# Folding eight heads' sums of 16 tokens on VectorE and by transfers instead of on TensorE

## The chip, the cores and the metric

The kernel runs on one core of a Trainium2 chip. The metric is the device time of one execution in microseconds (us). TensorE is the matrix engine, VectorE (DVE in the rows of the profile), ScalarE (ACT) and GpSimd (POOL) work on tiles of 128 partitions, and the DMA engines move data. SyncE (SP) and GpSimd issue most transfers. The engines run at once and wait for each other by semaphores; each works through its own instructions in the order in which they were written.

## The reference

One decoder layer over 256 tokens of width 1024. The first half (a projection, a retention branch, an attention branch, a gated merge) gives a residual stream x1. The second half adds to it a retrieval of single-neuron experts, and only this part matters here:

```python
q = (ht @ w_q).reshape(T, PEER_HEADS, 2, half)                  # 8 heads
...                                                             # top 16 of 128 * 128 experts for each head
def one_chunk(args):
    hc, ec, gc = args
    u = u_tab[ec]                                               # rows of a table of 16384 experts
    a = jax.nn.gelu(jnp.einsum('td,thkd->thk', hc, u), approximate=False)
    return jnp.einsum('thk,thkd->td', gc * a, v_tab[ec])        # sum over 8 heads and 16 experts of each
...
x = x + peer(h2, ...)
```

For each token, 8 heads x 16 experts give 128 rows of `peer_v` (1024 numbers each), which are summed with weights and added to x1.

## The kernel before

The kernel computes most tokens densely: a first product takes all 16384 rows of `peer_u` against the tokens, in 128 chunks of 128 rows; a second product multiplies the weights (zero where an expert was not chosen) with all rows of `peer_v`, again in 128 chunks. Some tokens are handled by gathering just the rows that they need. For the second product these are 64 tokens whose rows are summed in a tile `vacc`, and 16 more tokens whose rows are summed in a tile `accx`. This leaves `ND` = 176 tokens to the second product.

In `accx` the 128 partitions are 8 heads x 16 tokens: partition 16 h + i holds the sum over the 16 experts that head h chose for token i. Each `accx` step gathers one row per partition (an indirect DMA issued by GpSimd, line 1033) and adds it with a weight on VectorE (line 1119). The sums of the 8 heads remain to be added across partitions. TensorE does that: line 1348 multiplies each of the 8 column blocks of `accx` with `pick`, a 128 x 16 matrix of ones at the rows of each token, which gives the 16 tokens' sums as 16 more columns of the second product's result.

The second product (line 1320 on) is one loop over chunks c = 0 to 127. In its iteration c, in this order, the program

- asks SyncE for the next chunks of `peer_v` (512 KB each, into `raw_ring`, which holds 6),
- prepares chunk c + 2: ScalarE rounds it to `rhi` (line 147), VectorE takes the rest `rlo` = chunk - `rhi` (line 148), and for each second chunk the same is done for the weights in `cw` (lines 1256 and 1257),
- lets TensorE multiply chunk c: for each of 8 blocks of 128 columns one matmul of `rhi` (line 1316) and one of `rlo` (line 1317), into 8 banks of PSUM (named `side` or `acc`), where the sums stay over all chunks,
- takes 0.65 of a gather step: GpSimd issues the gather of one set of rows, and VectorE adds the oldest set that was gathered (six sets are in flight).

In six pairs of chunks (12 and 13, 32 and 33, 52 and 53, 72 and 73, 92 and 93, 112 and 113), called plain here, the chunk is not split: one matmul per block (line 1314), nothing to prepare.

At c = 123 all gather sums are done, the rows of x1 are fetched back (lines 1340 to 1346) and line 1348 runs. For the last two chunks the loop goes block by block: when a block is complete, ScalarE and VectorE add its two halves (lines 1360 and 1361), TensorE turns it back to token order (1366 and 1367), VectorE adds x1 (1368 and 1369), and the output is stored. In the tile `r0b`, which collects tokens 64 to 127, rows 48 to 63 are the 16 tokens of `accx`.

The order on each engine is simply that of the program; nothing reorders it later.

Of the kernel before, what the change touches and what calls it, by code (L numbers as in the profile page):

```python
# [11 lines left out]
F32 = mybir.dt.float32  # L12
# [6 lines left out]
AF = mybir.ActivationFunctionType  # L19
OP = mybir.AluOpType  # L20
AX = mybir.AxisListType

P = 128
S = 256
NT = S // P
D = 1024
KC = D // P
# [3 lines left out]
NG = 64  # L31
NXP = 16
# [3 lines left out]
NA = S - NG - NX  # L36
ND = S - NG - NXP * NXV
# [12 lines left out]
TOPK = 16  # L50
HELD = [0, 1, 2, 8, 14, 21] + list(range(26, 62, 6))
HELD0 = 14
NPRE = 16
STEP = 7
PRE0 = 20
# [6 lines left out]
NJ = NP // 2  # L62
NU = NJ + NX
NV = NJ + NXP * NXV
# [11 lines left out]
def layer_kernel(ctx, tc, x, mix_norm_g, w_in, ret_w_branch, moba_q_gain, moba_k_gain, moba_w_branch,  # L76
                 rel_bias, w_out, ffn_norm_g, peer_w_q, peer_sub_keys, peer_u, peer_v,
                 c_rope, c_decay, c_col, c_bucket, out, dbg=None):
    nc = tc.nc
    V, A, G, T = nc.vector, nc.scalar, nc.gpsimd, nc.tensor  # L80
    ctx.enter_context(tc.manual_schedule())

    cp = ctx.enter_context(tc.tile_pool(name="cp", bufs=1))
# [13 lines left out]
    def side():  # L97
        return psum.tile([P, 512], F32, name="side", bufs=4)
# [64 lines left out]
    x1d = dr.tile([P, NT, D], F32, name="x1d")  # L163
# [4 lines left out]
    hTf = cp.tile([P, KC, NA], F32, name="hTf")  # L168
    hh = [hp_.tile([P, 4, S], F32R, name="hh", bufs=2) for _ in range(2)]
    hl = [hp_.tile([P, 4, S], F32R, name="hl", bufs=2) for _ in range(2)]  # L170

    turned = dr.tile([NPRE, P, D], F32, name="turned")
    ident = cp.tile([P, P], F32, name="ident")
# [515 lines left out]
    def load_any(i):  # L689

        if sk_at <= i < sk_at + 2:
            r = raw_tile().rearrange("p (j i) -> p j i", j=H)
            nc.sync.dma_start(r, peer_sub_keys[0].rearrange("h c n d -> n (h c) d")[:, H * (i - sk_at):H * (i - sk_at + 1), :])
            sk_raw.append(r)
            return
        i -= 2 * (i >= sk_at)
        if i < len(pieces):
            load(i)
        elif i < len(pieces) + NK:
            c = i - len(pieces)  # L700
            if c in HELD:
                return
            if early_chunk(c):
                u_raw[c] = raw_tile()
                nc.sync.dma_start(u_raw[c], turned[c // STEP])
            elif c in TURN:
                u_raw[c] = raw_tile()
                load_quarters(nc.sync, u_raw[c], c)
            else:
                u_raw[c] = load_rows(peer_u, c)  # L710
        elif i < len(pieces) + 2 * NK:
            v_raw[i - len(pieces) - NK] = load_rows(peer_v, i - len(pieces) - NK)
# [4 lines left out]
    def load_to(i):  # L717
        while state["loaded"] < i + AHEAD + 2 * (i + AHEAD > sk_at):
            load_any(state["loaded"])
            state["loaded"] += 1  # L720
# [19 lines left out]
    def early_chunk(c):  # L740
        return c % STEP == STEP - 1 and c // STEP < NPRE

# [11 lines left out]
    def early_turns(i):  # L754

        m, step = divmod(i - PRE0, PERIOD)
        if step == 0 and -1 <= m < NPRE - 1:
            load_quarters(nc.scalar, early[0][(m + 1) % 2], STEP * (m + 1) + STEP - 1)
        if 0 <= m < NPRE:
            if step < 2:  # L760
# [33 lines left out]
    for t in range(NT):  # L794
        for q in range(2):
            c = slice(512 * q, 512 * (q + 1))
# [3 lines left out]
            p = side()  # L800
# [4 lines left out]
    for q in range(2):  # L805
        for t in range(NT):
            n = slice(t * P, (t + 1) * P)
            A.activation(hh[q][:, :, n], sides[2 * t + q], AF.Copy)
    for q in range(2):
        for t in range(NT):  # L810
            n = slice(t * P, (t + 1) * P)
# [50 lines left out]
    tk = ctx.enter_context(tc.tile_pool(name="tk", bufs=1))  # L862
# [43 lines left out]
    gs = {"n": 0, "u": 0, "dot": 0, "v": 0, "sum": 0, "rows": {}, "x": 0, "soft": False, "xdone": False, "later": [], "pace": GATHER}  # L906
# [1 line left out]
    topk_rest = []  # L908
    ready = []
    v_order = [*range(NJ, NV), *range(NJ)]  # L910
    pick = tk.tile([P, NXP], F32, name="pick")

    def x_rows(a, n):

# [204 lines left out]
                V.scalar_tensor_tensor(a, r, av[:, j:j + 1], a, op0=OP.mult, op1=OP.add)  # L1119
            gs["sum"] += 1  # L1120

    V.tensor_reduce(pick, ident.rearrange("p (h i) -> p i h", i=NXP), axis=AX.X, op=OP.add)
    V.tensor_copy(iota4, iota[:, :, None].to_broadcast([P, NK, 4]))
    held = list(HELD)

    def hold():
        n0, c = 1024 * (len(HELD) - len(held)), held.pop(0)
        u_raw[c] = W[:, HELD0:SCRATCH, :].rearrange("p c t -> p (c t)")[:, n0:n0 + D]
        nc.sync.dma_start(u_raw[c], peer_u[0, c * P:(c + 1) * P, :])
# [138 lines left out]
    for c in range(NK):  # L1268
# [13 lines left out]
        for k in range(KC):  # L1282
            n = c % 2 * NA
            T.matmul(pa[:, n:n + NA], uT[:, k * P:(k + 1) * P], hT[:, k], start=(c % 2 == 0 and k == 0),  # L1284
                     stop=(k == KC - 1), skip_group_check=True)
# [21 lines left out]
    o = [side() for _ in range(4)] + [acc(i) for i in (1, 1, 0, 0)]  # L1307
    half = P - NG
# [8 lines left out]
        T.matmul(o[b][:, :ND], vl[:, n], w[:, :ND], start=False, stop=(c == NK - 1), skip_group_check=True)  # L1317

    cuts = {}
    for c in range(NK):  # L1320
        load_to(len(pieces) + NK + c + 2)
        if (c + 2) // 2 not in PLAIN:
            cut_v(c + 2)
            if c % 2 == 0:
                cut_w(c + 2)
        if c // 2 in PLAIN:
            cuts[c] = (v_raw.pop(c), None, W[:, c, :])
        else:
            cuts[c] = (*v_cut.pop(c), w_cut[c - c % 2][:, c % 2])
        if c < NK - 2:  # L1330
            for b in range(KC):
                block(b, c)
            del cuts[c]
        gather(GATHER_V)
        if c == NK - 5:
            while gs["sum"] < NV:
                gather_step()

            r0 = tk.tile([P, D], F32, name="rows_", bufs=2)
            nc.gpsimd.dma_start(r0[:NG], x1d[:NG, 0, :])  # L1340
            upper = hp_.tile([P, D], F32, name="rows", tag="hh", bufs=2)
            r1 = hp_.tile([P, D], F32, name="rows", tag="hh", bufs=2)
            r0b = oh_more.rearrange("p a b i j -> p (a b i j)").bitcast(F32)
            nc.gpsimd.dma_start(r0b[:half], x1d[NG:, 0, :])
            nc.gpsimd.dma_start(r1, x1d[:, 1, :])
            nc.gpsimd.dma_start(upper[:NG], gs["acc"][NG:])
            for b in range(KC):
                T.matmul(o[b][:, 2 * ND:2 * ND + NXP], gs["accx"][:, b * P:(b + 1) * P], pick, start=False, stop=True,
                         skip_group_check=True)
        if c == NK - 2:  # L1350
            V.tensor_tensor(r0[:NG], r0[:NG], gs["acc"][:NG], op=OP.add)
        if c == NK - 1:
            V.tensor_tensor(r0[:NG], r0[:NG], upper[:NG], op=OP.add)
            nc.sync.dma_start(out_flat[:NG, :], r0[:NG])
# [2 lines left out]

    def add_up(b):
        t = back[b] = hp_.tile([P, 512], F32, name="turned", tag="hl", bufs=2)
        A.activation(t[:, :ND + NXP], o[b][:, ND:2 * ND + NXP], AF.Copy)  # L1360
        V.tensor_tensor(t[:, :ND], t[:, :ND], o[b][:, :ND], op=OP.add)

    def turn_back(b):
        t = back.pop(b)
        n = slice(b * P, (b + 1) * P)
        T.transpose(o[b][:, :P], t[:, :P], ident)
        T.transpose(o[b][:half, P:2 * P], t[:, P:P + half], ident)
        V.tensor_tensor(r1[:, n], r1[:, n], o[b][:, :P], op=OP.add)
        V.tensor_tensor(r0b[:half, n], r0b[:half, n], o[b][:half, P:2 * P], op=OP.add)
        if b in (3, 5, 7):  # L1370
            d = slice({3: 0, 5: 512, 7: 768}[b], P * (b + 1))
            nc.sync.dma_start(out_flat[P:, d], r1[:, d])
            q = nc.scalar if b == 7 else nc.sync
            q.dma_start(out_flat[NG:P, d], r0b[:half, d])
# [62 lines left out]
```

## Time and profile before

| | |
|---|---|
| median of 3 runs | 948.59 us (946.0 to 951.2) |
| the profiled execution's own time | 945.74 us |
| its span, first to last instruction | 944.0 us |
| TensorE busy | 935.0 us (99%) |
| VectorE busy | 792.2 us (84%) |
| GpSimd busy | 395.7 us (42%) |
| first and last matmul group of the second product (line 1316) | from 653.1 us to about 939 us |
| `accx` sums on VectorE (line 1119) | 659.7 to 709.4 us |
| line 1348 | 926.3 to 928.0 us |

Rows of the timeline give the start, the duration, the engine, the line, the operation and `output<-inputs` with shapes; the brackets at the end tell how long the engine was idle before and what released it. A number behind two underscores tells apart buffers of one name: `rhi__9302` and `rlo__9303` are the two halves of one chunk. VectorE and TensorE overlap the end of one instruction with the start of the next, so the difference of two starts is a better price than a duration.

### The profile page before, as it was taken

How to read it: one execution, taken by the hardware profiler on the slowest of the kernel's cores; microseconds unless marked ns; L12 is line 12 of the kernel's file. 1: busy time of each engine (PE TensorE's matmuls, PEld its weight loads, DVE VectorE, ACT ScalarE, POOL GpSimd, SP SyncE). 2: the span in 40 equal slices, each digit the busy share in tenths (PEclk: the TensorE clock that was granted, in tenths of full speed). 3: DMA queues.
4: the chain of work that ended last, by engine and by line, in shares of the span. 5: the costliest groups of instructions: out<-in, count | busy, mean ns of one | idle time of the engine just before them, and what ended most of it. 6: DMA issues, size and time to landing. Idle time of an engine off the chain costs nothing.

```text
span 944.0 us, 19147 instructions
## 1 busy us (share of the span) xinstructions
PE 935.0 (99%) x7208; PEld 896.5 (95%) x7208; DVE 792.2 (84%) x1514; ACT 522.7 (55%) x958; POOL 395.7 (42%) x306
## 2 busy tenths in 40 slices
PE   9999999999999999999999999999999999999998
PEld 6887898998999999999999999999999999999997
DVE  6657557778678999999988999974989999898987
ACT  6554645544544445434678777876454545364553
POOL 3422010000203446534556776763547656564720
PEclk9999999999999999999999999999999999999999
DMA  9878779998798998999999999998999999999993
GB/s 321 235 193 237 236 205 298 304 300 261 248 371 327 405 396 280 404 407 364 408 357 392 379 375 376 375 407 318 385 360 401 409 383 407 373 397 400 405 360 117
DMA packets 109419, 320.40 MB, mean 339 GB/s; under 512 B 11373, under 2 KB 22518, under 8 KB 109199
## 3 DMA queue, kind: packets, MB, share of 16 engines
q1 hardware_dynamic: 64492, 184.43, 54.8%
q0 software_dynamic: 32512, 115.54, 32.4%
q10 hardware_dynamic: 12322, 19.21, 6.8%
q8 instruction: 57, 0.93, 0.4%
q14 instruction: 36, 0.29, 0.1%
HBM read 307.52 MB, written 13.14 MB: 340 GB/s over the span
## 4 chain that ended last, share of the span: by engine, by line
PE 74%; DVE 15%; DMA 7%; ACT 1%; issue 1%; POOL 1%; SPq 0%; DVEq 0%; POOLq 0%; ACTq 0%
PE acc L1284 13%; PE acc L1316 9%; PE side L1316 9%; PE acc L230 6%; PE side L737 6%; PE acc L231 6%; PE acc L232 6%; PE acc L1317 4%; PE side L1317 4%; DVE rows L1044 3%; DMA raw_ring<-in_peer_w_q_dram 2%; PE acc L239 2%; PE acc L241 2%; PE acc L240 2%; PE side L1314 2%; PE acc L1314 2%
## 5 line engine op out<-in xcount | busy, mean ns | idle before, releaser
L1033 POOL DMA_INDIRECT rows<-in_peer_u_dram,eg x86 | 108.5, 1262 | 72.9 <-DVE rows L1044 34.0
L1033 POOL DMA_INDIRECT rows<-in_peer_v_dram,eg x54 | 100.2, 1856 | 67.1 <-DVE vacc L1119 45.7
L737 PE MATMUL side<-ident,raw_ring 128*128 128x128 f32 x800 | 107.2, 277 | 0.0
L737 PEld LDWEIGHTS side<-ident,raw_ring 128*128 128x128 f32 x800 | 97.0, 192 | 0.0
L1161 ACT ACTIVATE oh_buf<-oh_more,tS 128x128 bf16<-128x128 f16 x176 | 58.6, 420 | 0.0
L1044 DVE SCALAR_TENSOR_TENSOR rows<-rows,h 128x1024 f32<-128x1024 f32 x43 | 52.4, 1232 | 4.1 <-DMA rows<-in_peer_u_dram,eg 4.1
L1119 DVE SCALAR_TENSOR_TENSOR vacc<-rows,av,vacc 128x1024 f32<-128x1024 f32 x43 | 55.1, 1281 | 0.1
L1256 ACT ACTIVATE cw<-W 128x352 fp32r<-128x352 f32 x58 | 28.6, 494 | 47.6 <-PE acc L1317 38.5
L1242 POOL TENSOR_TENSOR W<-W,gl 128x256 f32<-128x256 f32 (+20 forms) x32 | 27.5, 861 | 46.3 <-ACT gl L1241 39.5
L1257 DVE TENSOR_TENSOR cw<-W,cw 128x352 fp32r<-128x352 f32 x58 | 30.3, 522 | 18.0 <-ACT cw L1256 18.0
L580 POOL DMA_DIRECT2D x1d<-xt x1 | 0.7, 657 | 88.5 <-DVE xt L562 88.5
L1156 DVE TENSOR_TENSOR oh_more<-iota,tI 128x1024 f16<-128x1024 f16 x44 | 34.5, 785 | 0.0
L1157 DVE TENSOR_TENSOR oh_buf<-oh_more,tM 128x1024 f16<-128x1024 f16 x44 | 32.6, 740 | 2.2
L154 POOL TENSOR_TENSOR gny<-va,minus_half 128x8 f32<-128x8 f32 x2 | 4.3, 2126 | 66.7 <-DVE va L454 66.7
L1284 PE MATMUL acc<-hTd,raw_ring 128*128 128x128 f32 x256 | 31.2, 275 | 0.0
L1284 PEld LDWEIGHTS acc<-hTd,raw_ring 128*128 128x128 f32 x256 | 29.9, 192 | 0.0
L1211 PE MATMUL acc<-oh_buf 128*128 128x128 bf16 x176 | 24.4, 219 | 0.0
L1212 PE MATMUL acc<-oh_buf 128*128 128x128 bf16 x176 | 24.4, 219 | 0.0
L1225 ACT ACTIVATE W<-acc 128x512 f32<-128x512 f32 (+21 forms) x44 | 17.3, 394 | 10.9 <-PE acc L1212 8.5
L1227 DVE TENSOR_TENSOR W<-acc,W 128x264 f32<-128x264 f32 (+20 forms) x32 | 16.1, 502 | 6.5 <-ACT W L1225 5.3
L1244 ACT ACTIVATE W<-acc 128x256 f32<-128x256 f32 (+20 forms) x52 | 18.4, 353 | 4.4 <-PE acc L1284 4.4
L1211 PEld LDWEIGHTS <-oh_buf 128*128 128x128 f16 x176 | 19.8, 114 | 0.0
(2701 smaller groups left out, 3486.4 us busy)
## 6 DMA issues: line engine op xcount, KB each, us to landing
raw_ring<-in_peer_v_dram SPq DMA_DIRECT2D x128, 512.0 KB
raw_ring<-in_peer_u_dram SPq DMA_DIRECT2D x100, 512.0 KB
raw_ring<-in_w_in_dram SPq DMA_DIRECT2D x52, 512.0 KB
raw_ring<-in_peer_w_q_dram SPq DMA_DIRECT2D x16, 512.0 KB
raw_ring<-turned SPq DMA_DIRECT2D x16, 512.0 KB
W<-in_peer_u_dram SPq DMA_DIRECT2D x12, 512.0 KB
eraw<-in_peer_u_dram ACTq DMA_DIRECT2D x32, 128.0 KB
h<-in_peer_u_dram ACTq DMA_DIRECT2D x32, 128.0 KB
```

The source lines that it names most:

```text
L230: T.matmul(o[t], xh[:, s], wh, start=(k == 0), stop=False)
L231: T.matmul(o[t], xh[:, s], wl, start=False, stop=False)
L232: T.matmul(o[t], xl[:, s], wh, start=False, stop=(k == kc - 1))
L737: T.transpose(p[:, k * P:(k + 1) * P], r.rearrange("p (i k) -> p k i", k=KC)[:, 4 * q + k], ident)
L1033: G.indirect_dma_start(out=r, out_offset=None, in_=tab, in_offset=bass.IndirectOffsetOnAxis(ap=eg[:, j:j + 1], axis=0))
L1044: V.scalar_tensor_tensor(r, r, 1.0, h, op0=OP.mult, op1=OP.mult, accum_out=av[:, j:j + 1])
L1119: V.scalar_tensor_tensor(a, r, av[:, j:j + 1], a, op0=OP.mult, op1=OP.add)
L1161: A.activation(o1[:, j], hot[:, 0, :, j], AF.Copy, scale=tS[:, t, k + j:k + j + 1])
L1211: T.matmul(p[:, j * P:(j + 1) * P], hi, o1, start=True, stop=False)
L1284: T.matmul(pa[:, n:n + NA], uT[:, k * P:(k + 1) * P], hT[:, k], start=(c % 2 == 0 and k == 0), stop=(k == KC - 1), skip_group_check=True)
L1316: T.matmul(o[b][:, :2 * ND], vh[:, n], w, start=(c == 0), stop=False, skip_group_check=True)
L1317: T.matmul(o[b][:, :ND], vl[:, n], w[:, :ND], start=False, stop=(c == NK - 1), skip_group_check=True)
```

## The change

The sum over the 8 heads leaves TensorE. After the gathers of `accx` are done, three halvings fold its partitions: a transfer copies the upper half of what is left to a tile `fold` (in the place of `hTf`, whose last use was in the first product), at partition 0 on, and VectorE adds it to the lower half. From 128 partitions this leaves 64, 32 and 16. A fourth step fetches the 16 tokens' x1 from DRAM to `fold` and adds it too. Each transfer is issued by GpSimd at c = 40, 56, 72 and 88, and each addition is written 8 chunks later, at c = 48, 64, 80 and 96. The 16 finished rows are copied to `r0b` at the end by one more transfer, in place of x1's rows there; the `pick` matrix, line 1348 and the 16 columns in what follows fall away.

```diff
+FOLD0 = 40
+FOLD = 8
...
-    pick = tk.tile([P, NXP], F32, name="pick")
...
-    V.tensor_reduce(pick, ident.rearrange("p (h i) -> p i h", i=NXP), axis=AX.X, op=OP.add)
...
     cuts = {}
+    fold = None
     for c in range(NK):
         load_to(len(pieces) + NK + c + 2)
+        m, step = divmod(c - FOLD0, 2 * FOLD)
+        if 0 <= m < 4 and step % FOLD == 0:
+            n, a = P >> m + 1, gs["accx"]
+            if c == FOLD0:
+                assert gs["sum"] >= NV - NJ
+                fold = cp.tile([P, D], F32, name="hTf")
+            if step == 0:
+                nc.gpsimd.dma_start(fold[:max(n, NXP)], a[n:2 * n] if n >= NXP else x1d[P - NXP:, 0, :])
+            else:
+                n = max(n, NXP)
+                V.tensor_tensor(a[:n], a[:n], fold[:n], op=OP.add)
         if (c + 2) // 2 not in PLAIN:
             cut_v(c + 2)
...
-            nc.gpsimd.dma_start(r0b[:half], x1d[NG:, 0, :])
+            nc.gpsimd.dma_start(r0b[:ND - NA], x1d[NG:P - NXP, 0, :])
+            nc.gpsimd.dma_start(r0b[ND - NA:half], gs["accx"][:NXP])
...
-            for b in range(KC):
-                T.matmul(o[b][:, 2 * ND:2 * ND + NXP], gs["accx"][:, b * P:(b + 1) * P], pick, start=False, stop=True,
-                         skip_group_check=True)
...
-        A.activation(t[:, :ND + NXP], o[b][:, ND:2 * ND + NXP], AF.Copy)
+        A.activation(t[:, :ND], o[b][:, ND:2 * ND], AF.Copy)
...
-        T.transpose(o[b][:half, P:2 * P], t[:, P:P + half], ident)
+        T.transpose(o[b][:ND - NA, P:2 * P], t[:, P:ND], ident)
...
-        V.tensor_tensor(r0b[:half, n], r0b[:half, n], o[b][:half, P:2 * P], op=OP.add)
+        V.tensor_tensor(r0b[:ND - NA, n], r0b[:ND - NA, n], o[b][:ND - NA, P:2 * P], op=OP.add)
```

On TensorE, between chunks 123 and 124, before:

```order
L1316 MATMUL acc<-cw,rhi__10225 128x352
L1317 MATMUL acc<-cw,rlo__10226 128x176
L1348 MATMUL side<-pick,accx 128x16 x4
L1348 MATMUL acc<-pick,accx 128x16 x4
L1316 MATMUL side<-cw,rhi__10247 128x352
L1317 MATMUL side<-cw,rlo__10248 128x176
```

and with the change:

```order
L1316 MATMUL acc<-cw,rhi__10232 128x352
L1317 MATMUL acc<-cw,rlo__10233 128x176
L1316 MATMUL side<-cw,rhi__10254 128x352
L1317 MATMUL side<-cw,rlo__10255 128x176
L1316 MATMUL side<-cw,rhi__10254 128x352
```

The eight matmuls of line 1348 are gone; the numbers of the buffers are 7 higher because more tiles were allotted before them.

On VectorE, the third addition stands in iteration c = 80, before chunk 82 is split. Before:

```order
L148 TENSOR_TENSOR rlo__9279<-raw_ring,rhi__9278 128x1024
L1119 SCALAR_TENSOR_TENSOR vacc<-rows__9123,av,vacc 128x1024
L148 TENSOR_TENSOR rlo__9303<-raw_ring,rhi__9302 128x1024
L1257 TENSOR_TENSOR cw<-W,cw 128x2x176
L148 TENSOR_TENSOR rlo__9326<-raw_ring,rhi__9325 128x1024
```

and with the change (lines 150 and 1120 are lines 148 and 1119 of before):

```order
L150 TENSOR_TENSOR rlo__9283<-raw_ring,rhi__9282 128x1024
L1120 SCALAR_TENSOR_TENSOR vacc<-rows__9126,av,vacc 128x1024
L1333 TENSOR_TENSOR accx<-accx,hTf 16x1024
L150 TENSOR_TENSOR rlo__9308<-raw_ring,rhi__9307 128x1024
L1257 TENSOR_TENSOR cw<-W,cw 128x2x176
L150 TENSOR_TENSOR rlo__9331<-raw_ring,rhi__9330 128x1024
```

The addition (16 partitions, `fold` shown by the name of its place, `hTf`) comes ahead of the split of chunk 82 and of the weights of chunks 82 and 83.

On GpSimd, the first two transfers stand among the gathers of line 1033, which is line 1034 of the change. With the change:

```order
L1034 DMA rows<-in_peer_v_dram,eg 128x1024 x3
L1330 DMA hTf<-accx 64x1024
L1034 DMA rows<-in_peer_v_dram,eg 128x1024
L1034 DMA rows__8465<-in_peer_v_dram,eg 128x1024
L1034 DMA rows__8512<-in_peer_v_dram,eg 128x1024
L1034 DMA rows<-in_peer_v_dram,eg 128x1024 x4
L1034 DMA rows__8671<-in_peer_v_dram,eg 128x1024
L1034 DMA rows__8702<-in_peer_v_dram,eg 128x1024
L1034 DMA rows<-in_peer_v_dram,eg 128x1024
L1330 DMA hTf<-accx 32x1024
```

Before, only the gathers stood there. The four transfers come after the 31st, 41st, 52nd and 62nd of the 80 gathers of `peer_v`.

## The prediction

> **What bounds the kernel now.** I read the page's busy times first, then a table by stretches of the second product, then the list of waits of TensorE there, and last the timeline around the instructions that change.
>
> ```profile
> PE 935.0 (99%) x7208; PEld 896.5 (95%) x7208; DVE 792.2 (84%) x1514; ACT 522.7 (55%) x958; POOL 395.7 (42%) x306
> ```
>
> ```profile
> core 0: us, PE busy (x) PEld busy (x) DVE busy (x) ACT busy (x) POOL busy (x), PEclk, DMA share, GB/s
> 655.00:765.00 110.00, 109.88 (x801) 109.67 (x800) 100.58 (x101) 58.76 (x71) 65.29 (x33) 1.00 1.00 385
> 765.00:860.00 95.00, 95.00 (x691) 95.00 (x690) 86.35 (x86) 47.92 (x59) 55.36 (x28) 1.00 1.00 390
> 860.00:925.00 65.00, 65.00 (x476) 65.00 (x475) 59.38 (x60) 34.33 (x41) 30.21 (x17) 1.00 1.00 379
> ```
>
> TensorE is busy without a gap through the second product at its full clock (1.00). Two other things are nearly full as well: VectorE works 246.3 of these 270 us, and the DMA share is 1.00. In the whole stage TensorE waits hardly at all. The list of its waits from 653 us on has two rows, both in the last blocks:
>
> ```profile
> PE acc L1366 <- DVE turned L1361: 0.3, 1, 0.3
> PE side L1366 <- DVE turned L1361: 0.3, 1, 0.3
> ```
>
> and the view of line 1316 shows one more, early in the product:
>
> ```profile
> its engine sat idle before it (us, times) until:
>   DVE cw L1257: 0.3, 1
> ```
>
> So TensorE's work sets the end: work taken from it is gained, and work given to VectorE or to the DMA engines costs nothing as long as they stay ahead of TensorE. By how much they are ahead is the question.
>
> **What is removed from TensorE.**
>
> ```profile
> 926.05 0.35 PE L1316 MATMUL acc<-cw,rhi__10225 128*128 128x352 f32 x1
> ...
> 926.32 0.99 PE L1348 MATMUL side<-pick,accx 128*128 128x16 f32 x8
> 927.16 1.04 PE L1348 MATMUL acc<-pick,accx 128*128 128x16 f32 x8
> 928.05 0.41 PE L1316 MATMUL side<-cw,rhi__10247 128*128 128x352 f32 x1
> ...
> 928.37 0.36 PE L1316 MATMUL side<-cw,rhi__10247 128*128 128x352 f32 x1
> ```
>
> Pairs of matmuls of lines 1316 and 1317 start 0.27 us apart (926.05 to 926.32, where the next pair would have stood). The next pair starts at 928.05, so line 1348 takes 928.05 - 926.32 = 1.73 us, and the pair behind it takes 928.37 - 928.05 = 0.32 instead of 0.27. Together 1.78 us are removed. Does everything behind move up with it? Chunks 124 and 125 need nothing new. The first block of the tail does:
>
> ```profile
> 929.35 1.21 DVE L1351 TENSOR_TENSOR rows__10290<-rows__10290,vacc 64x1024 f32<-64x1024 f32 x1
> 930.60 1.22 DVE L1353 TENSOR_TENSOR rows__10290<-rows__10290,rows 64x1024 f32<-64x1024 f32 x1
> 933.57 0.34 DVE L1361 TENSOR_TENSOR turned<-turned,side 128x176 f32<-128x176 f32 x1 [1.75 <-ACT turned L1360]
> ...
> 933.21 0.33 ACT L1360 ACTIVATE turned<-side 128x192 f32<-128x192 f32 x1 [5.19 <-PE side L1317]
> ```
>
> VectorE waits 1.75 us for ScalarE there after line 1353, which ends at 931.82. Moved up by 1.78 us, line 1361 would start at 931.79: the idle time is used up, but no more than 0.03 us is lost. I take the whole 1.78 us as gained.
>
> **What else shrinks.** Line 1360 copies 176 instead of 192 columns, at most 16/192 of 0.33 us = 0.03 us each, eight times: 0 to 0.2 us, and since only some of them are on the chain at the end I take 0.05 us. The turned blocks and the last additions lose partitions, not columns; an addition over 64 partitions (1.21 us above) costs as much as one over 128 (1.22 us in line 148's rows below), so nothing there. The addition that made `pick` was 0.37 us in a stretch where VectorE then waits 3.66 us:
>
> ```profile
> 252.51 0.37 DVE L1122 TENSOR_REDUCE pick<-ident 128x16 f32<-128x128 f32 x1 [1.22 <-PE side L604]
> 252.80 0.41 DVE L1123 CAST iota<-iota 128x512 f16<-128x512 f32 x1
> 256.88 1.22 DVE L148 TENSOR_TENSOR rlo__2485<-raw_ring,rhi__2484 128x1024 fp32r<-128x1024 f32 x1 [3.66 <-ACT rhi__2484 L147]
> ```
>
> No gain there: the wait for the load that follows ends when it ends.
>
> **The four additions.** Each has 1024 columns of f32, like line 1351, whose start lies 1.25 us before the next; line 148 takes 1.13 us so. I take 1.2 us, 4.8 us in all. VectorE works in order, so each addition delays the preparation of the next chunks by 1.2 us until VectorE next has idle time. What counts is how long before TensorE's need that preparation ends. The two rows that matter are line 1257 (the weights `cw` of a pair of chunks) and TensorE's first matmul of that pair. The reference for no margin is the one place where TensorE did wait:
>
> ```profile
> 701.21 0.52 DVE L1257 TENSOR_TENSOR cw<-W,cw 128x352 fp32r<-128x352 f32 x1
> ...
> 701.78 0.43 PE L1316 MATMUL side<-cw,rhi__7942 128*128 128x352 f32 x1
> ```
>
> It ended at 701.73 and TensorE started 0.05 us later. At the four places where the additions come, ahead of chunks 50, 66, 82 and 98:
>
> ```profile
> 760.68 0.53 DVE L1257 TENSOR_TENSOR cw<-W,cw 128x352 fp32r<-128x352 f32 x1
> ...
> 763.32 0.35 PE L1316 MATMUL side<-cw,rhi__8587 128*128 128x352 f32 x1
> ...
> 795.15 0.52 DVE L1257 TENSOR_TENSOR cw<-W,cw 128x352 fp32r<-128x352 f32 x1
> ...
> 798.62 0.35 PE L1316 MATMUL side<-cw,rhi__8943 128*128 128x352 f32 x1
> ...
> 832.06 1.22 DVE L148 TENSOR_TENSOR rlo__9303<-raw_ring,rhi__9302 128x1024 fp32r<-128x1024 f32 x1
> 833.19 0.52 DVE L1257 TENSOR_TENSOR cw<-W,cw 128x352 fp32r<-128x352 f32 x1
> ...
> 833.92 0.35 PE L1316 MATMUL side<-cw,rhi__9302 128*128 128x352 f32 x1
> ...
> 865.57 1.23 DVE L148 TENSOR_TENSOR rlo__9659<-raw_ring,rhi__9658 128x1024 fp32r<-128x1024 f32 x1 [1.86 <-ACT rhi__9658 L147]
> ```
>
> Ahead of chunk 50 the weights are ready 763.32 - 761.21 = 2.1 us early, ahead of chunk 66 2.95 us: 1.2 us fit in. Ahead of chunk 98 VectorE is idle for 1.86 us anyway, waiting for a load: the addition fits into that. Ahead of chunk 82 the weights end at 833.71 and are used at 833.92, 0.21 us later, of which 0.05 us is no margin. There TensorE must wait 1.2 - 0.16 = 1.04 us. Once it has waited, VectorE is ahead again and the chunks behind find their weights ready. So the additions cost 1.04 us; the bounds are 0 (if that stretch has the margin of the others) and 4.8 us (if all four have none).
>
> **The transfers.** 64, 32, 16 and 16 rows of 4 KB make 512 KB, beside the same bytes for x1 as before.
>
> ```profile
> 740.77 1.68 POOL L1033 DMA_INDIRECT rows<-in_peer_v_dram,eg  x1 [2.32 <-DVE vacc L1119]
> ...
> 796.78 2.03 POOL L1033 DMA_INDIRECT rows<-in_peer_v_dram,eg  x1 [0.30 <-issue]
> ...
> 808.23 1.28 DVE L1119 SCALAR_TENSOR_TENSOR vacc<-rows,av,vacc 128x1024 f32<-128x1024 f32 x1
> ...
> 907.46 0.54 POOL L1344 DMA_DIRECT2D oh_more<-x1d  x1
> ```
>
> Issuing one takes GpSimd about 0.54 us (line 1344), ahead of the next gather; a gather is issued 11 us or more before its rows are read (the tightest case is in the rows above), so nothing waits for half a microsecond. Would VectorE wait for the folded rows? The first is issued behind the gather of 740.77, so at about 743, and read at about 759.5: 16 us later. A gather twice as large, issued at 796.78, was read at 808.23 (the two rows are matched by counting back from the last gather and the last sum) without a wait, 11.5 us later, in the full DMA stream. So the new wait of VectorE is not expected to hold; cost 0.
>
> The transfers also take DMA time from the loads of `peer_v`:
>
> ```profile
> 922.00:924.00 2.00, 2.00 (x17) 2.00 (x16) 2.00 (x3) 1.70 (x3) 0.00 (x0) 1.00 0.89 354
> 926.00:928.00 2.00, 2.00 (x20) 2.00 (x18) 2.00 (x3) 1.43 (x2) 0.42 (x1) 1.00 0.55 121
> ```
>
> At the rate of the first row (354 GB/s at a share of 0.89, 398 GB/s when full) 512 KB are 1.3 us. The second row holds a copy of 64 rows from one half of the partitions to the other (line 1346), the nearest thing to a fold: 121 GB/s at 0.55 is 220 GB/s when full, and 512 KB are 2.4 us. Spread over four places where VectorE is 2 to 3 us ahead or the transfer falls behind a plain pair, I take 0, with bounds 0 and 2.4 us.
>
> [...]
>
> **Sum.** -1.78 - 0.05 + 1.04 + 0 = -0.8 us. The profiled execution took 945.74 us (944.0 us of span and 1.7 us around it), so it would take 944.9. The median of the three runs lies 2.85 us higher, for which the trace of the fastest has no row; applying the difference to the median gives 947.8 us.
>
> **Rivals.** (a) All is hidden. The thin margin at chunk 82 is an accident: at chunk 80 a load came late, and in the three other stretches the weights are 1 to 3 us early. Without that wait the change gains 1.83 us: 946.8 us. Against it: the thin stretch comes just behind a plain pair, where loads bunch, and such bunching will be there in other executions too.
>
> (b) Slower: VectorE has no margin at any of the four places. The mechanism is one: the median execution is 2.85 us slower than the profiled one, and if late loads make that up, VectorE runs just ahead of TensorE everywhere, so that each addition and the transfers' DMA time reach TensorE. This decides when the margins of 2.1 and 2.95 us fall under 1.2 us. Price: 4.8 + 2.4 - 1.83 = +5.4 us, 954.0 us; with the additions alone +3.0, 951.6. For it speaks the DMA share of 1.00; against it that VectorE has 24 us of idle time in the stage.
>
> (c) The removal is lost in the tail. With line 1348 gone the tail's first block comes when lines 1351 and 1353 still run (0.03 us by the rows above). If VectorE reaches these lines later than in this trace, the tail waits for them: the gain of 1.78 us goes, and with the wait at chunk 82 the time is 948.59 - 0.05 + 1.04 = 949.6 us.
>
> **How the numbers follow.** Forecast 0.47, (a) 0.32, (b) 0.12, (c) 0.09. About 0.5% (4.7 us) is what a measurement of this kernel can tell from no change: its three runs already lie 0.5% apart. Forecast, (a) and (c) are within it; the scatter of a median puts 0.07 of their weight below the lower bound and 0.02 above the upper one; of (b) half lies beyond. So faster 0.07, same 0.85, slower 0.08. The range, 944.0 to 952.0 us, holds the forecast and (a) with the runs' scatter of some 2.5 us, and (b) at the price of its additions.
>
> **What would show it.** In the changed kernel's profile: no row between chunks 123 and 124; four additions of 1.2 us on VectorE, none with idle time before it put down to a transfer; TensorE's list of waits with one new row, on the `cw` of one pair behind the third or another addition, of about 1 us. Several such rows would be (b), none (a); idle time ahead of line 1361's first row that is put down to VectorE's own queue would be (c). I am wrong about the mechanism if TensorE waits for anything else, or if VectorE waits for a folded row.

## The result, and the profile after

The changed kernel takes 955.58 us (median of 22 runs, 949.3 to 966.2), the kernel before 946.91 on the same chips: the ratio is 1.0089, with a 95% interval of 1.0067 to 1.0111. It is slower by 8 us where 0.8 us less was forecast, and it lies outside the range. Ratios here and below leave out disturbed runs, so a ratio can lie under the quotient of the two medians.

The profiled execution took 956.66 us (span 954.9), 10.9 more than the one before. The first matmul of the second product and the first that turns a finished tile back in the tail cut this in three. From the timelines, before:

```profile
653.06 0.41 PE L1316 MATMUL side<-cw,rhi__7447 128*128 128x352 f32 x1
...
933.96 0.33 PE L1366 MATMUL side<-ident,turned 128*128 128x128 f32 x1 [0.26 <-DVE turned L1361]
```

and after:

```profile
656.42 0.41 PE L1316 MATMUL side<-cw,rhi__7445 128*128 128x352 f32 x1
...
944.91 0.33 PE L1376 MATMUL side<-ident,turned 128*128 128x128 f32 x1 [1.51 <-DVE turned L1371]
```

The second product starts 3.4 us later, long before the first transfer or addition: over the 14 profiles of this study that start lies anywhere from 651.8 to 656.4, and the run with the short copy below, the same program up to there, starts at 651.8. The stretch up to the first turned tile grew from 280.9 to 288.5 us, and these 7.6 us are what has to be explained. TensorE's list of waits in that stage had two rows of 0.3 us before. Now:

```profile
PE side L1316 <- DVE cw L1257: 5.5, 5, 2.4
PE side L1376 <- DVE turned L1371: 1.5, 1, 1.5
PE acc L1376 <- DVE turned L1371: 0.3, 1, 0.3
```

Neither of the first two rows was forecast at this size. What is VectorE late for? Not for a folded row: line 1333, the addition, never waits. GpSimd's row for the gathers of `peer_v` (lowest, middle and highest duration of one issue, in ns) tells more, before and after:

```profile
L1033 POOL DMA_INDIRECT rows<-in_peer_v_dram,eg x51: 937/1683/3598, 654.7 to 904.1; - x51
```

```profile
L1034 POOL DMA_INDIRECT rows<-in_peer_v_dram,eg x51: 937/1681/16888, 658.1 to 912.8; - x51
```

The middle issue is unchanged, but one takes 16.9 us. Three of the issues in the timeline of GpSimd are longer than any of the second product before (4.56 us at most, in a row of its own):

```profile
762.19 6.77 POOL L1034 DMA_INDIRECT rows<-in_peer_v_dram,eg  x1 [0.66 <-DVE vacc L1120]
...
798.65 16.89 POOL L1034 DMA_INDIRECT rows<-in_peer_v_dram,eg  x1 [0.65 <-DVE vacc L1120]
...
838.95 5.57 POOL L1034 DMA_INDIRECT rows__9350<-in_peer_v_dram,eg  x1 [0.65 <-DVE vacc L1120]
```

Each lies across one of the additions (at 761.84, 799.42 and 838.59, 1.2 us each). VectorE's rows around the longest:

```profile
799.42 1.20 DVE L1333 TENSOR_TENSOR accx<-accx,hTf 32x1024 f32<-32x1024 f32 x1
...
813.46 1.27 DVE L1120 SCALAR_TENSOR_TENSOR vacc<-rows__8920,av,vacc 128x1024 f32<-128x1024 f32 x1
820.59 1.28 DVE L1120 SCALAR_TENSOR_TENSOR vacc<-rows,av,vacc 128x1024 f32<-128x1024 f32 x1 [5.87 <-DMA rows<-in_peer_v_dram,eg]
```

From the addition to 814.73 there are 15 instructions, each recorded as starting before the one ahead of it has ended. GpSimd's issue ends at 815.54, some 0.8 us after that run, about as long as an issue takes by itself (0.94). By then VectorE has used up all rows gathered earlier and stands still for 5.87 us until the late one lands. TensorE runs dry behind it:

```profile
823.50 0.44 PE L1316 MATMUL side<-cw,rhi__9131 128*128 128x352 f32 x1 [2.39 <-DVE cw L1257]
```

And then TensorE is slow. The table by stretches (PEclk, the granted clock, is the third number from the end, ahead of the DMA share and the GB/s):

```profile
822.00:824.00 2.00, 0.50 (x3) 0.51 (x4) 2.00 (x3) 0.00 (x0) 1.69 (x3) 1.00 1.01 387
824.00:826.00 2.00, 2.00 (x12) 2.00 (x11) 2.00 (x3) 0.00 (x0) 1.42 (x1) 0.64 1.03 420
826.00:828.00 2.00, 2.00 (x9) 2.00 (x9) 2.00 (x3) 1.06 (x1) 1.96 (x1) 0.51 1.03 418
828.00:830.00 2.00, 2.00 (x16) 2.00 (x16) 2.00 (x3) 0.27 (x1) 1.35 (x2) 1.00 1.03 414
```

The granted clock falls to 0.64 and 0.51 for two stretches of 2 us: 0.72 + 0.98 = 1.7 us lost. The account of the 7.6 us is then: waits 5.5 + 1.5 less the 0.5 of before, minus 1.8 for line 1348, plus 1.7 for the clock, 6.4 in all; 1.2 us have no row that I can name. Of the 5.5 us, 1.81 stand near the end (at 928), behind loads of v for which ScalarE had to wait 3.41 us; whether the gathers that were issued late, in a burst, delayed these loads, no run shows. The run with idle time below has TensorE waits of 0.69 and 0.49 us near the same place (at 919 and 924) without one long issue, so a part of them need not come of the long issues.

### The profile page after: what moved, and what is told of

Same layout as the page of the kernel before. It is cut to its first block, busy times and chain, and to the rows that moved or that the text cites. A ratio compares the mean times of both kernels' runs of the same rounds, so it can differ in the third digit from the quotient of the medians.

```text
span 954.9 us, 19128 instructions
## 1 busy us (share of the span) xinstructions
PE 937.0 (98%) x7192; PEld 898.1 (94%) x7192; DVE 796.5 (83%) x1517; ACT 521.5 (55%) x958; POOL 412.1 (43%) x311
## 4 chain that ended last, share of the span: by engine, by line
PE 71%; DVE 19%; DMA 6%; issue 2%; POOL 1%; ACT 1%; SPq 0%; DVEq 0%; POOLq 0%; ACTq 0%
PE acc L1284 13%; PE acc L1316 7%; PE side L1316 7%; PE acc L232 6%; PE side L739 6%; PE acc L233 6%; PE acc L234 6%; DVE rows L1045 4%; PE acc L1317 3%; PE side L1317 3%; PE acc L241 2%; PE acc L243 2%; PE acc L242 2%; DMA rows<-in_peer_v_dram,eg 2%; DMA raw_ring<-in_peer_v_dram 2%
## 5 line engine op out<-in xcount | busy, mean ns | idle before, releaser
L1034 POOL DMA_INDIRECT rows<-in_peer_v_dram,eg x54 | 116.5, 2158 | 62.7 <-DVE vacc L1120 45.0
```

The source lines that it names most:

```text
L1034: G.indirect_dma_start(out=r, out_offset=None, in_=tab, in_offset=bass.IndirectOffsetOnAxis(ap=eg[:, j:j + 1], axis=0))
```

## Experiments

Theory A: behind an extra instruction VectorE runs without a gap, GpSimd cannot issue the next gather in that time, and the late row stalls VectorE and TensorE. Theory B: VectorE is late by the additions' own time, no more. Theory C: the transfers delay other transfers. Theory D: removing line 1348 does it. Each kernel was timed beside the kernel before, and the ratios are to that. Some expectations split theory A into A1 and A2; what these letters stand for differs from run to run and is said in each.

### The additions alone

```
+            if step == FOLD:
+                n = max(n, NXP)
+                V.tensor_tensor(fold[:n], a[:n], a[:n], op=OP.add)
```

> The kernel before, with four extra VectorE additions at the places where the change adds the folded rows (chunks 48, 64, 80, 96; 64, 32, 16 and 16 partitions of 1024). They write into a tile that nothing reads, so no fold transfer is issued, and line 1348 stays on TensorE. Theory A (an addition of 1.2 us closes VectorE's gaps, a gather's issue on GpSimd then waits for VectorE's unbroken run, and the late rows stall VectorE and TensorE): about the changed kernel's 955.6 plus the 1.8 of line 1348, 954 to 959, with at least one gather issue of over 5 us right at an addition and a VectorE wait of some us for a gathered row. Theory B (each addition makes VectorE late by its own 1.2 us and no more): 948 to 951.6, no gather issue over 4.6 us. Theory C (the fold transfers delay the loads of v or the gathers): 946 to 948, since there are none. Theory D (removing line 1348, or the renamed tiles, shift the tail): 946 to 948.

961.46 us, ratio 1.0156 (1.0121 to 1.0191): the whole loss without one fold transfer, and more than A's upper bound. VectorE's and GpSimd's rows at the third place:

```profile
834.45 1.21 DVE L1333 TENSOR_TENSOR hTf<-accx 16x1024 f32<-16x1024 f32 x1
...
859.82 1.28 DVE L1121 SCALAR_TENSOR_TENSOR vacc<-rows__9349,av,vacc 128x1024 f32<-128x1024 f32 x1 [5.78 <-DMA rows__9349<-in_peer_v_dram,eg]
```

```profile
834.81 20.06 POOL L1035 DMA_INDIRECT rows__9349<-in_peer_v_dram,eg  x1 [0.66 <-DVE vacc L1121]
```

The row whose issue took 20.06 us (`rows__9349`) is the very row for which VectorE then waits. C and D fall as the cause, and B, which has no such issue.

### The transfers alone

```
+            if step == 0:
+                nc.gpsimd.dma_start(fold[:max(n, NXP)], a[n:2 * n] if n >= NXP else x1d[P - NXP:, 0, :])
```

> The kernel before, with the four fold transfers alone (issued by GpSimd at chunks 40, 56, 72, 88, into a tile that nothing reads); no additions, and line 1348 stays on TensorE. Theory A: 946 to 948, gather issues no longer than before (4.6 us at most). Theory B: 946 to 948. Theory C: 954 to 957, with loads of v or gathers that land later behind the fold transfers. Theory D: 946 to 948.

945.65 us, ratio 0.9994 (0.9974 to 1.0014), and no gather's issue is long:

```profile
L1035 POOL DMA_INDIRECT rows<-in_peer_v_dram,eg x51: 949/1687/3257, 657.0 to 906.0; - x51
```

The transfers cost nothing that can be measured, as forecast.

### The additions next to the plain pairs

```
-FOLD = 8
+FOLD = 11
+EVERY = 20
...
-        m, step = divmod(c - FOLD0, 2 * FOLD)
+        m, step = divmod(c - FOLD0, EVERY)
```

> The changed kernel with the same transfers and additions at other chunks: transfers at 40, 60, 80, 100, additions at 51, 71, 91, 111. Each addition then falls where the next pair of chunks is used uncut, so that VectorE has two cuts (2 x 1.22 us) less to do right there. Theory A and theory B both say that the loss goes: 944 to 947 (the kernel before less up to 1.8 for line 1348), and A adds that no gather issue is longer than about 5 us. Theory C and theory D: about 955, as the transfers and the removal are the same.

946.58 us, ratio 0.9994 (0.9973 to 1.0014). The same work at other chunks, with line 1348 gone, costs nothing that can be measured. The issue behind the first addition:

```profile
763.79 2.87 POOL L1035 DMA_INDIRECT rows__8671<-in_peer_v_dram,eg  x1 [0.66 <-DVE vacc L1121]
```

VectorE has less to do there and comes to a gap at 765.85, and the issue is over 0.81 us later. (Against A's expectation, one issue of 6.77 us remains, at the last place; nothing waits for it.) But why is there no gain, with line 1348 gone? VectorE's rows in the tail, and TensorE's behind them:

```profile
930.27 1.21 DVE L1362 TENSOR_TENSOR rows__10297<-rows__10297,vacc 64x1024 f32<-64x1024 f32 x1
931.52 1.22 DVE L1364 TENSOR_TENSOR rows__10297<-rows__10297,rows 64x1024 f32<-64x1024 f32 x1
932.66 0.57 DVE L1372 TENSOR_TENSOR turned<-turned,side 128x176 f32<-128x176 f32 x2
```

```profile
933.04 0.33 PE L1377 MATMUL side<-ident,turned 128*128 128x128 f32 x1 [1.73 <-DVE turned L1372]
```

TensorE arrives earlier and waits 1.73 us for VectorE, which has just done its two additions onto the first 64 rows of the output.

### A sum along the row in place of each addition

```
-                V.tensor_tensor(fold[:n], a[:n], a[:n], op=OP.add)
+                V.tensor_reduce(fold[:n, :1], a[:n], axis=AX.X, op=OP.add)
```

> As the run with the additions alone, but each of the four additions is replaced by a VectorE sum along the row of the same tile (64, 32, 16, 16 partitions of 1024 to one column), which reads one operand in place of two and should take about the same 1.1 to 1.2 us; its result is not read. Theory A1 (any VectorE work of that length closes the gaps): as with the additions, 954 to 959, gather issues of over 5 us at the same places. Theory A2 (only an operation with two operands in the on-chip memory holds GpSimd's issue back, the others let it in): 946 to 950, and a gather issue pending at one of the four ends when the row sum begins. Theory B: as with the additions alone. Theory C and D: 946 to 948.

954.95 us, runs from 946.6 to 966.2, ratio 1.0045 (1.0011 to 1.0078). It takes 1.20 us as the addition does, and issues of 6.76, 14.91 and 5.56 us lie across or behind three of the four; the first:

```profile
757.83 1.20 DVE L1333 TENSOR_REDUCE hTf<-accx 64x1 f32<-64x1024 f32 x1
```

```profile
758.18 6.76 POOL L1035 DMA_INDIRECT rows<-in_peer_v_dram,eg  x1 [0.64 <-DVE vacc L1121]
```

An instruction with one operand in place of two brings the long issues too. Whether it costs less than an addition is not clear from runs so far apart.

### A short copy behind the additions

Behind the cuts of the chunk that has the addition:

```
+        if 0 <= m < 4 and step == FOLD:
+            V.tensor_copy(fold[:1, :1], v_cut[c + 2][1][:1, :1].bitcast(F32))
```

> The changed kernel with one small VectorE operation more behind each of the four additions: after the cuts of the same chunk it copies one element of the cut just made, so that VectorE has to wait until its own last result is written, a gap of some hundredths of a microsecond (the gap that ended one of the long issues in the changed kernel was 0.03 us). It takes no work away and makes VectorE a little later. Theory A (the long issues come from VectorE's run without a gap): 946 to 950, and no gather issue of over 5 us near an addition. Theory B (what counts is that VectorE is late by 1.2 us and that rows come late for it): 955 to 957, the long issues stay.

957.80 us, ratio 1.0129 (1.0091 to 1.0167), issues of 16.96 and 20.11 us. The edit failed to do what it was for: the copy starts at 795.28, the next sum at 795.34, and the copy's row ends at 795.42, so there is no gap. The run tells nothing against A, and nothing for it.

### The additions behind the cuts

The same four lines, moved behind `cut_v` and `cut_w` of the chunk.

> The changed kernel with each of the four additions put after the cuts of its chunk in place of before them. In the changed kernel an addition follows a sum directly, so that the gather which the sum has released waits on GpSimd while the addition runs; here it has one or two cuts in which it can get in first. Theory A1 (shut out is the issue that is pending when the addition starts): 946 to 950, no gather issue of over 5 us. Theory A2 (VectorE that is late by an addition shuts out every issue until it next has a gap, wherever the addition is): 953 to 960, with issues of over 5 us behind the additions.

958.05 us, ratio 1.0136 (1.0104 to 1.0169). From the timelines of VectorE and GpSimd, at the fourth place:

```profile
870.36 1.21 DVE L1337 TENSOR_TENSOR accx<-accx,hTf 16x1024 f32<-16x1024 f32 x1
...
897.39 1.28 DVE L1120 SCALAR_TENSOR_TENSOR vacc<-rows__9734,av,vacc 128x1024 f32<-128x1024 f32 x1 [6.69 <-DMA rows__9734<-in_peer_v_dram,eg]
```

```profile
873.03 18.49 POOL L1034 DMA_INDIRECT rows__9734<-in_peer_v_dram,eg  x1 [4.64 <-DVE vacc L1120]
```

This issue began 1.5 us after the addition had ended. So it need not be pending while the addition runs (A1 of this run falls): the addition changes what comes behind it, and the issue waits until VectorE next has a gap (at 890.70; the issue is over at 891.52; A2 of this run holds).

### Line 1348 left out, and nothing in its place

The changed kernel without the lines of `fold`: the sums of eight heads are left unadded for the 16 tokens. What it measures is the removal alone.

> The changed kernel without fold transfers and additions: the eight heads' sums of the 16 tokens are left unadded (only the first head's 16 rows reach the output, so the output of the last 16 tokens lacks the other seven heads). What is left of the change is the removal of line 1348 and the narrower tail. By the forecast's term for that removal: 945.1 (before less 1.78), TensorE not waiting at the first turned tile. By the rival that the removal is lost in the tail, where VectorE's two 1.2 us additions on the first 64 rows of the output come next: 946.5 to 947.3, TensorE waiting about 1.7 us for the first turned tile.

944.63 us, ratio 0.9986 (0.9967 to 1.0006): anything from a gain of 3 us to none, which by the time tells neither expectation from the other. TensorE's first wait in the tail is there again:

```profile
PE side L1364 <- DVE turned L1359: 1.4, 1, 1.4
```

The timelines of TensorE tell more. From the last block of chunk 123 to the first turned tile it took 7.91 us before (926.05 to 933.96), 7.22 here (931.00 to 938.22), 7.39 in the changed kernel (937.52 to 944.91) and 8.05 with the additions at the plain pairs (924.99 to 933.04). Of the 1.78 us, 0.7, 0.5 and nothing arrived in these three executions.

### Plain pairs, and one of the tail's additions earlier

```
+        if c == 104:
+            nc.gpsimd.dma_start(fold[NG:], x1d[:NG, 0, :])
+        if c == 110:
+            V.tensor_tensor(gs["acc"][NG:], gs["acc"][NG:], fold[NG:], op=OP.add)
...
-            nc.gpsimd.dma_start(r0[:NG], x1d[:NG, 0, :])
...
-        if c == NK - 2:
-            V.tensor_tensor(r0[:NG], r0[:NG], gs["acc"][:NG], op=OP.add)
...
-            V.tensor_tensor(r0[:NG], r0[:NG], upper[:NG], op=OP.add)
+            V.tensor_tensor(r0[:NG], upper[:NG], gs["acc"][:NG], op=OP.add)
```

> The kernel with the additions at the plain pairs, and one thing more: the first of VectorE's two additions in the tail (the residual rows onto the 64 rows of sums) is made at chunk 110, next to a plain pair, into the other half of the sums, so that only one addition of 1.2 us is left in the tail. If VectorE's two additions set the wait of 1.7 us for the first turned tile, the wait falls to about 0.5 us and the time to 945.0 to 946 (1.2 below the additions at the plain pairs, 946.6, and the only version expected below the kernel before); if something else sets the end, 946.6.

944.93 us, ratio 0.9991 (0.9976 to 1.0007). The wait is gone (0.27 us are left), but others stand ahead of it:

```profile
PE side L1317 <- DVE cw L1258: 1.7, 3, 0.8
PE acc L1378 <- DVE turned L1373: 0.3, 1, 0.3
```

The lowest median beside the last, but not measurably faster than the kernel before.

### A real gap behind the additions

In `gather_step`, behind the issue of a gather and ahead of the next sum, once after each addition (which sets the flag):

```
             gs["v"] += 1
+            if gs.pop("shake", None):
+                G.memset(shake[:1, :1], 0.0)
+                V.tensor_copy(shake[:1, 1:2], shake[:1, :1])
```

> The changed kernel in which VectorE, once behind each of the four additions, waits until GpSimd has issued the gather that is pending at that time (GpSimd clears one element behind the issue, VectorE copies it ahead of its next sum). VectorE does the same additions and is held up by a further 1 to 1.5 us at each of four places, four to six in all. Theory A (the run without a gap shuts the issue out, and a real gap ends that state): the long issues go (none over 5 us within 20 us of an addition), no VectorE wait of over 5 us for a row, 946.5 to 951. Theory A2 (VectorE's being late keeps issues out, gap or not): the pending issue gets in at the gap, but one of the next is long again; 953 to 960. Theory B (VectorE's lateness itself is the price): 956 to 961.

950.71 us, ratio 1.0022 (1.0001 to 1.0043): VectorE does the same additions and is held up on top of them at two of the four places, and three quarters of the loss are gone (0.22% in place of 0.89%). One execution shows a place with the gap and one without. VectorE and GpSimd at the first place, where the copy did wait:

```profile
758.87 1.21 DVE L1338 TENSOR_TENSOR accx<-accx,hTf 64x1024 f32<-64x1024 f32 x1
...
762.58 0.14 DVE L1115 COPY shake<-shake 1x1 f32<-1x1 f32 x1 [0.94 <-POOL shake L1114]
```

```profile
759.22 3.24 POOL L1034 DMA_INDIRECT rows<-in_peer_v_dram,eg  x1 [0.66 <-DVE vacc L1125]
...
764.22 1.69 POOL L1034 DMA_INDIRECT rows<-in_peer_v_dram,eg  x1 [1.67 <-DVE vacc L1125]
```

and at the second, where GpSimd had cleared its element already and the copy found nothing to wait for:

```profile
795.19 1.21 DVE L1338 TENSOR_TENSOR accx<-accx,hTf 32x1024 f32<-32x1024 f32 x1
...
797.90 0.13 DVE L1115 COPY shake<-shake 1x1 f32<-1x1 f32 x1
```

```profile
799.50 11.88 POOL L1034 DMA_INDIRECT rows<-in_peer_v_dram,eg  x1 [3.31 <-DVE vacc L1125]
```

At the first place the pending issue, of 6.77 us in the changed kernel, is over after 3.24, some 0.8 us behind VectorE's stop, and the next takes its usual 1.69, though VectorE is later than ever. The third place, with a gap of 0.94 us as well, has 4.37 and then 1.68 us. At the second, without a gap, the issue takes 11.88 (16.89 in the changed kernel). At the fourth the copy found nothing to wait for either, but VectorE had just stood still for 1.45 us behind a load, and no issue is long. So a gap ends it, which lateness by itself (A2 of this run, and B) does not explain. The expectation that none is long was wrong only where no gap came about.

### Idle time in place of the additions

The kernel before with the same four holds, without transfers and additions.

> The kernel before, in which VectorE idles at the four places instead of adding: it waits, ahead of a sum, until GpSimd has issued the gather pending at that time, some 1 to 1.5 us each, about as long as an addition (1.2 us). No transfers, no additions, line 1348 on TensorE. Theory A (only a run without a gap shuts the issue out): 946 to 949.5, no gather issue over 5 us. Theory A2 (VectorE late by that much, whatever it did in that time, shuts out the issues that follow): 952 to 960, with issues of over 5 us behind the four places. Theory B: 948 to 952, no long issues.

949.57 us, ratio 1.0027 (1.0005 to 1.0049), no issue over 4.13 us. VectorE's list of waits has the holds:

```profile
DVE shake L1116 <- POOL shake L1115: 3.4, 3, 1.5
```

Being late by 1.1 us at three places costs 2.6 us (0.5 to 4.6), at the edge of A's range and inside B's. These holds come to 3.4 us, against the additions' 4.8, so mere time may have cost a little more than that; the additions alone cost 14.

### The additions in quarters

```
+        if 0 <= m < 4 and FOLD <= step < FOLD + 4:
+            n, a, d = max(P >> m + 1, NXP), gs["accx"], slice((step - FOLD) * (D // 4), (step - FOLD + 1) * (D // 4))
+            V.tensor_tensor(a[:n, d], a[:n, d], fold[:n, d], op=OP.add)
```

> The changed kernel with each addition cut into four of 256 columns, one in each of four chunks in a row (48 to 51, 64 to 67, 80 to 83, 96 to 99), so that VectorE is late by about 0.33 us at a time in place of 1.2. VectorE's whole time for the folds is a little more than before. Theory A and A2 (the state lasts until VectorE has caught up, which it does in the time between if it is little late): 945 to 948, no gather issue over 5 us, or few. Theory that VectorE's total time counts: 955 or more.

963.39 us, ratio 1.0189 (1.0138 to 1.0240): the slowest of all, against my expectation. A quarter takes 0.41 us, and behind the last of them, at 881.10, an issue takes 18.80 us:

```profile
881.45 18.80 POOL L1034 DMA_INDIRECT rows__9770<-in_peer_v_dram,eg  x1 [2.95 <-DVE vacc L1120]
```

```profile
907.22 1.28 DVE L1120 SCALAR_TENSOR_TENSOR vacc<-rows__9770,av,vacc 128x1024 f32<-128x1024 f32 x1 [7.78 <-DMA rows__9770<-in_peer_v_dram,eg]
```

The size of one piece is not what counts: short pieces bring the long issues as whole additions do. The time lies where the theory that VectorE's total time counts had put it (955 or more), but the pieces take only 0.2 us more than an addition at each place, from start to start, and the idle time above cost 2.6 us in all.

### One addition

```
+            if c == 64:
+                V.tensor_tensor(fold[:n], a[:n], a[:n], op=OP.add)
```

> The kernel before with one extra VectorE addition alone, at chunk 64 (the second place), into a tile that nothing reads; the run with all four cost 14 us. If the price is an issue that is shut out for a long time, one place can carry much of it: an issue of 12 to 20 us behind the addition, a VectorE wait of 5 us or more for the row, 951 to 957. If each addition costs its own time and margin, a quarter of the 14: 949.5 to 951.5 with no such wait.

950.33 us, ratio 1.0054 (1.0026 to 1.0083), with the long issue and the wait that A names:

```profile
790.07 17.03 POOL L1035 DMA_INDIRECT rows__8919<-in_peer_v_dram,eg  x1 [2.10 <-DVE cw L1259]
```

```profile
812.83 1.28 DVE L1121 SCALAR_TENSOR_TENSOR vacc<-rows__8919,av,vacc 128x1024 f32<-128x1024 f32 x1 [6.55 <-DMA rows__8919<-in_peer_v_dram,eg]
```

About 5 us, a third of the four additions' 14. The median lies in the range of the second expectation, the long issue and the wait are those of the first. This issue began 2.1 us ahead of the addition (at 792.17). The same gather before:

```profile
791.91 4.56 POOL L1033 DMA_INDIRECT rows__8918<-in_peer_v_dram,eg  x1 [3.57 <-DVE cw L1257]
```

```profile
795.58 1.28 DVE L1119 SCALAR_TENSOR_TENSOR vacc<-rows,av,vacc 128x1024 f32<-128x1024 f32 x1
```

It was over 0.89 us after the start of the next sum, and VectorE had no gap there: its rows overlap from 787.77 to 808.19, and this issue and four more got in during that time. With the addition the next sum (at 794.88) and all others up to the gap at 806.29 passed without letting the issue in. So a run without a gap is not enough to shut an issue out; the extra instruction changes what happens at the sums behind it.

## Why the prediction was wrong

**What bounds the kernel.** Right as far as it went: VectorE's margin decides. It left out that VectorE's work also decides when GpSimd gets to issue a gather.

**The removal of line 1348.** TensorE does lose it, but the 1.78 us did not arrive. The step "no more than 0.03 us is lost" failed: TensorE waits 1.51 us for the first turned tile (1.73 with the additions at the plain pairs, 0.26 before), and by the timelines 0 to 0.7 us of the gain arrived there. The trace of before had VectorE 1.75 us early there, and I kept its two additions onto the first 64 rows where that trace has them, ending 5.77 us behind the start of the last block of chunk 123. With line 1348 left out they ended 6.92 us behind it, in the changed kernel 7.09, with the additions at the plain pairs 7.75: VectorE's margin in the tail was that of one execution. Its work there stands behind loads, which did not come earlier: at the plain pairs it last waited for ScalarE, and ScalarE for a load, ahead of 921.2, and then worked with hardly a pause up to the turned tile. This is the mechanism of rival (c), given 0.09. In the measured time the price of the line stays open between 0 and 3 us.

**The four additions.** Their duration was right (1.20 to 1.21 us), their cost wrong: 1.04 us in the sum, 14 (11.5 to 18) in the run with the additions alone. The step that failed is "Once it has waited, VectorE is ahead again and the chunks behind find their weights ready", with its 1.04 us at chunk 82. TensorE's list has no wait there at all; the great loss came behind chunk 66, which had the largest of the margins that it worked out, 2.95 us. The margin in `cw` was the wrong measure: what ran out was the store of gathered rows, five sums later.

**The transfers.** Right: 0, by the run with the transfers alone. But the sentence "nothing waits for half a microsecond" took GpSimd's issue time as a constant. The trace of before already showed it from 0.94 to 4.56 us, nearly every end in step with an instruction of VectorE (0.90 us behind a start, or 0.81 behind the start of a gap), and I had quoted a 2.03 us issue without asking what made it twice as long as the shortest.

**The rivals.** (b) had the right sign and nearly the right size (954.0), by the wrong mechanism: it needed margins under 1.2 us at all four places and late folds. Idle time in the additions' place cost 2.6 us, where (b) had 4.8 for the additions.

## What to carry to other kernels

Idle time of an engine that is not the bottleneck can be what lets another engine get on with its own work: before filling it, look at how long the other's instructions take and at which instants they end. Where GpSimd issues the transfers that VectorE lives on, put added VectorE work where VectorE comes to a gap soon after (next to the plain pairs the four additions cost nothing that could be measured, ratio 0.9994; elsewhere, alone, 14 us), and count how many buffers bridge the longest issue. And work taken off the bottleneck just ahead of a tail is worth only what the next engines in the tail can follow (here 0 to 0.7 us of 1.78).

## What the runs showed of the hardware

An issue of a gather on GpSimd took 0.94 us while VectorE stood still (four in a row from 815.85 on in the changed kernel) and up to 20.11 us beside VectorE (with the short copy). Twelve of the issues of over 5 us in the second product can be set against VectorE's rows: three in the changed kernel, two with the additions alone, one with one addition, three with the row sums, two with the additions behind the cuts, one with the quarters. Of these 11 ended 0.81 to 0.83 us after VectorE had come to a gap (the other is the 5.56 us of the row sums); 0.03 us between two sums were enough (768.14 to 768.17 in the changed kernel, issue over at 768.96). So the two engines get in each other's way here, and for longer than one instruction: a sum on VectorE lasts 1.28 us, and the longest issue of the changed kernel was kept out across 15 instructions. By what means, no run shows. What stays open: in ordinary stretches VectorE's rows overlap just as closely, and yet an issue mostly gets in soon after, ending 0.90 us behind the start of a row of VectorE (the median issue of before takes 1.68 us). In the long stretches the rows are some 0.01 us shorter (1.21 for a cut, 1.27 for a sum, against 1.22 and 1.28), from about the added instruction to the gap, but what lies behind that is only to be guessed; no run separated it.

TensorE's granted clock dropped to about a half for some 4 us behind a pause of 2.39 us (0.64 and 0.51 above), and in the run with one addition behind one of 2.53 us:

```profile
818.00:820.00 2.00, 2.00 (x10) 2.00 (x9) 2.00 (x3) 0.00 (x0) 0.01 (x1) 0.50 1.05 424
820.00:822.00 2.00, 2.00 (x12) 2.00 (x11) 2.00 (x3) 0.37 (x1) 1.69 (x1) 0.66 1.00 399
```

A pause of 1.81 us at 926 in the changed kernel left it at 1.00; one of 1.83 us in the run with the row sums did not (it ends at 817.48):

```profile
815.00:820.00 5.00, 3.17 (x18) 2.90 (x17) 5.00 (x6) 0.00 (x0) 2.66 (x2) 0.84 0.97 361
820.00:825.00 5.00, 5.00 (x32) 5.00 (x32) 5.00 (x6) 2.37 (x3) 3.35 (x2) 0.82 1.03 415
```

Other stretches agree: with the additions alone the clock was 0.66 over the 5 us behind one stall (820 to 825) and 0.64 and 0.67 over 10 us at another (860 to 870); a pause of 1.51 us at 943 in the changed kernel, and waits of up to 1.6 us with the gap for the issue, left it at 1.00. No run varied the length by itself, so whether it alone decides stays open. The stall of 2.39 us in the changed kernel cost a further 1.7 by this clock.
